# PEER gates: the second index's one-hot made by the scalar engine, and a bank of gates laid out with its tokens side by side

## The chip, the cores and the metric

One Trainium2 chip, one core. The metric is the device time of one execution, in microseconds.

## The reference

A decoder trunk of two layers on 256 tokens with 1024 channels. The change lies in the expert mixer (PEER), which both layers have. Cut to that:

```python
def peer_ffn(hn, wq, subkeys, u_tab, v_tab):
    q = (hn @ wq).reshape(B, T, 8, 2, 64)
    s = jnp.einsum('bthsd,hskd->bthsk', q, subkeys)
    s_top, i_top = lax.top_k(s, 16)
    cand = s_top[..., 0, :, None] + s_top[..., 1, None, :]
    c_top, c_idx = lax.top_k(cand.reshape(B, T, 8, 256), 16)
    i1 = jnp.take_along_axis(i_top[..., 0, :], c_idx // 16, axis=-1)
    i2 = jnp.take_along_axis(i_top[..., 1, :], c_idx % 16, axis=-1)
    expert = i1 * 128 + i2
    gate = jax.nn.softmax(c_top, axis=-1)
    ...
    act = jax.nn.gelu(jnp.einsum('cd,ckd->ck', xc, u_tab[expert]))
    return jnp.einsum('ck,ckd->cd', gate * act, v_tab[expert])
```

Each token has 8 heads x 16 = 128 chosen experts (i1, i2) of 128 x 128, each with a gate.

## The kernel before

The tokens are split. The last 96 are done sparsely: their rows of the tables are gathered by indirect DMA, 128 rows of 4 KB at a time, and DVE multiplies them (class `Sparse`: `fetch` L1310 on POOL, `one` L1337 for u and L1347 for v). The first 160 (`ND`) are done densely: PE multiplies them with all 16384 experts, in 128 blocks of 512 KB of the u table (`u_dense` L248), ScalarE applies gelu (`evac` L1004) into `z` (two tiles `z[0]`, `z[1]` of 64 blocks each, 128 partitions by 64 by 160 tokens), z is multiplied by a mask that holds each token's gates and is zero elsewhere, and PE multiplies z with the 128 blocks of the v table (`v_dense` L1011).

**The mask** is what `gates` makes, 64 blocks (half `hf`) at a time. For a token, entry (i2, i1) of the mask is the sum over its 128 choices of onehot(i2) x gate x onehot(i1): a matmul with the choices on the partitions. `turned` has put the indices and gates with choices on the partitions and tokens in the columns: `i1T`, `i2T`, and the gate as a sum of two fp16 numbers, `gHL`. The work goes in sets of four tokens (`GT`), 40 sets per half. Per set, DVE compares an iota with i2 (L1223, `o2`), with i1 (L1225, `o1`) and multiplies the latter with the two parts of the gate (L1227, `og`). ScalarE converts `o2` to fp8 and turns it so that a token's 128 entries lie together (L1231, `o8`). Four sets later, PE makes a bank of eight tokens (two sets): for each token two matmuls with `o8` as weights and `og` as moving operand, 64 columns out (L1242); at the next set DVE multiplies the bank into z (L1247, the weighing).

**What sets the order.** Within the u and v blocks all engines run in the order in which the code issues. The loop of `peer_and_ple` gives routing and gates a budget per block: a block gives `GATE_NS` = 950, a set uses up 1150, so there is about one set for 1.2 blocks. The gates of the first half are made during u blocks 65 to 127, those of the second half during v blocks 0 to 63:

```python
            if i == HB + 1:
                main.append(self.gates(0, z, l))
            sparse.step(base + i)
            step(self.GATE_NS if i > HB else self.DENSE_NS if sparse.ready else self.ROUTE_NS)
            ps = self.u_dense(base + i, hn)
```

The blocks come through a ring of 10 buffers of 512 KB, filled by SP as PE frees them (`raw_done`, `refill`, `fetch` L166). The gathers have 7 row buffers; `step` spreads them evenly over the blocks and ties the issue of each to the end of a dense block:

```python
        if i in k.last_mm:
            k.tc.add_manual_dep(ins.ins, k.last_mm[i].ins.name, mybir.DependencyInfo(
```

Of the kernel before, what the change touches and what calls it, by code (L numbers as in the profile page):

```python
# [11 lines left out]
F8 = mybir.dt.float8e4  # L12
# [8 lines left out]
T = 256  # L21
# [34 lines left out]
class Trunk:  # L56
# [13 lines left out]
    def setup(self):  # L70
# [34 lines left out]
        self.i2T = per.tile([128, ND], F16, name="i2T")  # L105
# [1067 lines left out]
    def turned(self, rp, fin, gate):  # L1173
# [20 lines left out]
        for i, (t0, n, _) in enumerate(TILES):  # L1194
            s = slice(t0, t0 + n)
            nc.scalar.activation(self.i1T[:, s], b[i][:, 0:n], AF.Copy)
            nc.scalar.activation(self.i2T[:, s], b[i][:, n:2 * n], AF.Copy)

            gs = rp.tile([128, 128], F32, name="rt_gs")[:, :n]
            nc.vector.tensor_scalar(gs, b[i][:, 2 * n:3 * n], GSCALE, None, op0=ALU.mult)  # L1200
            nc.vector.tensor_copy(self.gHL[:, 0, s], gs)
            nc.vector.tensor_tensor(out=self.gHL[:, 1, s], in0=gs, in1=self.gHL[:, 0, s],
                                    op=ALU.subtract)
        yield 1000

    def gates(self, hf, z, l):
# [8 lines left out]
        for i in range(n + lag):  # L1215
            if i < n:
                s = slice(i * GT, i * GT + GT)
                o2, og = [self.strm.tile([128, T], F32, name="sq", bufs=11).bitcast(F16)
                          for _ in range(2)]
                o2 = o2.rearrange("p (e t) -> p e t", t=GT)  # L1220
                og = og.rearrange("p (a e t) -> p a e t", a=2, t=GT)
                o1 = self.strm.tile([128, HB, GT], F16, name="o1", bufs=1)
                tt_(out=o2, in0=self.iota, in1=self.i2T[:, None, s].to_broadcast([128, 128, GT]),  # L1223
                    op=ALU.is_equal)
# [5 lines left out]
                o8 = self.rows.tile([128, GT, 128], F8, name="o8", bufs=6)  # L1230
                nc.scalar.activation(o8.rearrange("p t e -> p e t"), o2, AF.Copy,  # L1231
                                     saturate=False)
                sets[i] = (o8, og)
            k, at = divmod(i - lag, bank)
            if k >= 0 and at == 0:
                ps[k] = self.bank("g", 2)
                for j in range(bank):
                    o8, og = sets.pop(k * bank + j)
                    for t in range(GT):
                        c = (j * GT + t) * HB  # L1240
                        for p in range(2):
                            nc.tensor.matmul(ps[k][:, c:c + HB], o8[:, t], og[:, p, :, t],  # L1242
                                             start=p == 0, stop=p == 1)

            if k >= 0 and at == 1:
                v = z[hf][:, :, k * 8:k * 8 + 8].rearrange("p b t -> p t b")
                nc.vector.scalar_tensor_tensor(v, ps.pop(k).rearrange("p (t b) -> p t b", b=HB),  # L1247
# [201 lines left out]
```

## Time and profile before

| | before |
|---|---|
| median of 3 runs | 1523.9 us (1522.53 to 1526.96) |
| profiled execution | 1528.51 us, its span 1526.7 us |
| PE busy | 1500.7 us, 98% of the span |
| DVE busy | 1140.0 us, 75%, 2749 instructions |
| ACT busy | 684.7 us, 45%, 864 instructions |
| DMA | 514.83 MB, 337 GB/s over the span |
| chain that ended last, by engine | PE 67%, DVE 18%, DMA 13% |
| the gates' matmuls (L1242) | x1280, 5% of the chain |

Times are microseconds unless marked ns. An engine's busy time is a share of a span with several stages, so the stretches have to be read one by one; the chain is followed back from the last instruction to what released each step. PE's matmuls overlap in their pipeline, so their rate is the distance from start to start, not the duration of one.

### The profile page before, as it was taken

To read this page: it belongs to the slowest core of one execution; us is meant where nothing else is said; L and a number is where in the kernel's file an instruction comes from. 1 tells how busy PE (TensorE), PEld (TensorE's weight loads), DVE (VectorE), ACT (ScalarE), POOL (GpSimd) and SP (SyncE) were. 2 spreads that over 40 slices of the span, in tenths; PEclk is the share of its full clock that TensorE was granted. 3 is DMA by queue.
4 is the path that set the end of the run, shared out by engine and by line. 5 is a ranking of instruction groups with operands and counts; after the bars stand their busy time and mean duration, and the time that the engine had idled before them with its cause. 6 is when DMAs were issued, how large, how long until landed. Compare 5 with 4: busy or idle time off the path is not lost.

```text
span 1526.7 us, 30307 instructions
## 1 busy us (share of the span) xinstructions
PE 1500.7 (98%) x11910; PEld 1459.3 (96%) x11910; DVE 1140.0 (75%) x2749; ACT 684.7 (45%) x864; POOL 448.4 (29%) x406
## 2 busy tenths in 40 slices
PE   8999999999999999999999999999999999999997
PEld 8858999999999999999999999999999999999997
DVE  6997699988886888645448699988886788544446
ACT  6478321348873877000027321248872877000025
POOL 0000013343444333444400004343444333443400
PEclk9999999999999999999999999999999999999998
DMA  6603679999999999999994379999999999999980
GB/s 240 231 1 113 232 234 408 408 408 408 408 392 394 404 381 373 408 409 409 409 358 153 117 232 402 408 408 408 409 395 392 408 377 374 407 409 409 408 316 28
DMA packets 141246, 514.83 MB, mean 337 GB/s; under 512 B 15985, under 2 KB 16241, under 8 KB 140593
## 3 DMA queue, kind: packets, MB, share of 16 engines
q1 hardware_dynamic: 84384, 308.42, 52.7%
q0 software_dynamic: 55568, 202.66, 33.8%
q8 instruction: 94, 1.54, 0.4%
q10 hardware_dynamic: 1152, 1.82, 0.4%
q14 instruction: 48, 0.39, 0.1%
HBM read 511.53 MB, written 1.05 MB: 336 GB/s over the span
## 4 chain that ended last, share of the span: by engine, by line
PE 67%; DVE 18%; DMA 13%; issue 1%; ACT 1%; SPq 0%; ACTq 0%; DVEq 0%
PE bank_a L1011 27%; PE bank_a L248 19%; DMA wx<-in_v 10%; PE bank_g L1242 5%; DVE row L1337 4%; PE bank_a L225 3%; PE bank_a L227 3%; PE bank_a L226 3%; DVE rt_tmp L1029 2%; DMA wx<-in_u 1%; PE bank_a L564 1%; DVE rt_ixd L1033 1%; DVE rt_eq L1165 1%; DVE rt_eq L1161 1%; PE bank_a L635 1%
## 5 line engine op out<-in xcount | busy, mean ns | idle before, releaser
L1011 PE MATMUL bank_a<-z,wx 128*128 128x160 f32 x4096 | 576.1, 301 | 2.9
L248 PE MATMUL bank_a<-hn,wx 128*128 128x160 f32 x4096 | 569.4, 300 | 2.4 <-DVE rt_gs L1200 1.2
L1011 PEld LDWEIGHTS bank_a<-z,wx 128*128 128x128 f32 x4096 | 561.0, 191 | 10.0 <-DMA wx<-in_v 9.7
L248 PEld LDWEIGHTS bank_a<-hn,wx 128*128 128x128 f32 x4096 | 558.7, 190 | 4.9 <-DVE rt_gs L1200 1.7
L1231 ACT ACTIVATE o<-sq 128x512 fp8e4<-128x512 f16 x160 | 398.8, 2602 | 46.7 <-DVE sq L1223 46.5
L1310 POOL DMA_INDIRECT row<-in_ur,sp_idx x192 | 228.4, 1190 | 453.0 <-PE bank_a L248 175.9
L1347 DVE SCALAR_TENSOR_TENSOR sp_acc<-row,sp_w,sp_acc 128x1024 f32<-128x1024 f32 x188 | 241.7, 1286 | 152.3 <-DMA row<-in_v,sp_idx 151.6
L1310 POOL DMA_INDIRECT row<-in_v,sp_idx x192 | 212.0, 1104 | 332.6 <-PE bank_a L1011 215.4
L1337 DVE SCALAR_TENSOR_TENSOR row<-row,sp_x 128x1024 f32<-128x1024 f32 x192 | 231.4, 1218 | 32.1 <-DMA row<-in_ur,sp_idx 31.9
L184 ACT ACTIVATE wH<-wx 128x1024 fp32r<-128x1024 f32 (+1 forms) x63 | 65.4, 1042 | 387.8 <-DMA wx<-in_proj 336.4
L1004 ACT ACTIVATE z<-bank_a 128x160 f32<-128x160 f32 x256 | 96.3, 381 | 284.1 <-PE bank_a L248 283.5
L1247 DVE SCALAR_TENSOR_TENSOR z<-bank_g,z 128x512 f32<-128x512 f32 x80 | 93.1, 1164 | 65.5 <-PE bank_g L1242 65.5
L197 DVE TENSOR_TENSOR wL<-wx,wH 128x1024 fp32r<-128x1024 f32 (+1 forms) x63 | 75.9, 1206 | 51.5 <-ACT wH L184 51.0
L225 PE MATMUL bank_a<-hnH,wH 128*128 128x256 f32 x320 | 93.0, 294 | 6.5 <-ACT wH L184 6.0
L227 PE MATMUL bank_a<-hnH,wL 128*128 128x256 f32 x320 | 92.5, 290 | 0.3 <-DVE wL L197 0.3
L226 PE MATMUL bank_a<-hnL,wH 128*128 128x256 f32 x320 | 92.3, 289 | 0.0
L1242 PE MATMUL bank_g<-sq,o 128*128 128x64 f16 x1280 | 89.5, 237 | 0.0
L1242 PEld LDWEIGHTS <-o 128*128 128x128 fp8e4 x1280 | 82.6, 113 | 3.0
L1227 DVE TENSOR_TENSOR sq<-o,gHL 128x512 f16<-128x512 f16 x160 | 68.1, 426 | 11.1
L225 PEld LDWEIGHTS bank_a<-hnH,wH 128*128 128x128 f32 x320 | 62.8, 198 | 7.3 <-ACT wH L184 6.2
L1223 DVE TENSOR_TENSOR sq<-iota,i2T 128x512 f16<-128x512 f16 x160 | 67.3, 421 | 0.0
L227 PEld LDWEIGHTS bank_a<-hnH,wL 128*128 128x128 f32 x320 | 63.0, 197 | 0.7 <-DVE wL L197 0.6
(311 smaller groups left out, 1212.5 us busy)
## 6 DMA issues: line engine op xcount, KB each, us to landing
wx<-in_u SPq DMA_DIRECT2D x256, 512.0 KB, 12.2
wx<-in_v SPq DMA_DIRECT2D x256, 512.0 KB, 11.6
wx<-in_wq SPq DMA_DIRECT2D x16, 512.0 KB, 4.3
wx<-in_gatew SPq DMA_DIRECT2D x16, 512.0 KB, 6.4
wx<-in_win SPq DMA_DIRECT2D x15, 512.0 KB, 4.9
w<-in_cw SPq DMA_DIRECT2D x2, 2048.0 KB
wx<-in_wout SPq DMA_DIRECT2D x8, 512.0 KB, 3.5
row<-in_ur,sp_idx POOLq DMA_INDIRECT x192, 9.6
```

Of the source, the lines that this page charges most:

```text
L225: mm(out, wH, xH, start=start, stop=False, **kw)
L226: mm(out, wH, xL, start=False, stop=False, **kw)
L227: mm(out, wL, xH, start=False, stop=stop, **kw)
L248: m = self.nc.tensor.matmul(out, w[:, kt * 128:kt * 128 + 128], x[:, kt, :ND], start=kt == 0, stop=kt == KT - 1)
L1004: self.nc.scalar.activation(z[i // HB][:, i % HB], ps, AF.Gelu_apprx_tanh)
L1011: m = self.nc.tensor.matmul(acc[kt // 2][:, (kt % 2) * ND:(kt % 2) * ND + ND], w[:, kt * 128:kt * 128 + 128], x, start=b == 0 and kt % 2 == 0,
L1231: nc.scalar.activation(o8.rearrange("p t e -> p e t"), o2, AF.Copy, saturate=False)
L1242: nc.tensor.matmul(ps[k][:, c:c + HB], o8[:, t], og[:, p, :, t], start=p == 0, stop=p == 1)
L1247: nc.vector.scalar_tensor_tensor(v, ps.pop(k).rearrange("p (t b) -> p t b", b=HB), 1.0 / GSCALE, v, op0=ALU.mult, op1=ALU.mult)
L1310: ins = k.nc.gpsimd.indirect_dma_start(out=G, out_offset=None, in_=table, in_offset=bass.IndirectOffsetOnAxis(ap=self.idx[:, c:c + 1], axi ...
L1337: nc.vector.scalar_tensor_tensor(G, G, 1.0, self.x[u], op0=ALU.mult, op1=ALU.mult, accum_out=self.dot[:, col])
L1347: nc.vector.scalar_tensor_tensor(self.acc[u], G, self.w[:, col], self.acc[u], op0=ALU.mult, op1=ALU.add)
```

## The change

The comparison of the second index leaves VectorE. ScalarE makes the one-hot in two steps: for each of the four tokens Abs(iota - i2), with the negated index (`i2n`, now fp32) as bias of each partition, then one Relu(1 - that) over the four. The result is fp16, with a token's 128 entries together, and goes to PE as weights as it is; the conversion to fp8 is gone. The matmul's 64 columns are written eight elements apart in the bank, so that the eight tokens of a block lie side by side, and the weighing reads the bank in order and z in runs of eight.

```diff
-        self.i2T = per.tile([128, ND], F16, name="i2T")
+        self.i2n = per.tile([128, ND], F32, name="i2n")
...
-            nc.scalar.activation(self.i2T[:, s], b[i][:, n:2 * n], AF.Copy)
+            nc.scalar.activation(self.i2n[:, s], b[i][:, n:2 * n], AF.Copy, scale=-1.0)
...
-                o2, og = [self.strm.tile([128, T], F32, name="sq", bufs=11).bitcast(F16)
-                          for _ in range(2)]
-                o2 = o2.rearrange("p (e t) -> p e t", t=GT)
+                og = self.strm.tile([128, T], F32, name="sq", bufs=11).bitcast(F16)
                 og = og.rearrange("p (a e t) -> p a e t", a=2, t=GT)
                 o1 = self.strm.tile([128, HB, GT], F16, name="o1", bufs=1)
-                tt_(out=o2, in0=self.iota, in1=self.i2T[:, None, s].to_broadcast([128, 128, GT]),
-                    op=ALU.is_equal)
...
-                o8 = self.rows.tile([128, GT, 128], F8, name="o8", bufs=6)
-                nc.scalar.activation(o8.rearrange("p t e -> p e t"), o2, AF.Copy,
-                                     saturate=False)
-                sets[i] = (o8, og)
+                ab = self.rows.tile([128, 512], F16, name="ab", bufs=2)
+                for t in range(GT):
+                    nc.scalar.activation(ab[:, t * 128:t * 128 + 128], self.iota[:, :, 0], AF.Abs,
+                                         bias=self.i2n[:, i * GT + t:i * GT + t + 1])
+                o2 = self.strm.tile([128, T], F32, name="sq", bufs=11).bitcast(F16)
+                nc.scalar.activation(o2, ab, AF.Relu, scale=-1.0, bias=self.ones[:, 0:1])
+                sets[i] = (o2.rearrange("p (t e) -> p t e", t=GT), og)
...
-                    o8, og = sets.pop(k * bank + j)
+                    o2, og = sets.pop(k * bank + j)
                     for t in range(GT):
-                        c = (j * GT + t) * HB
+                        o = ps[k].rearrange("p (b t) -> p t b", b=HB)[:, j * GT + t]
                         for p in range(2):
-                            nc.tensor.matmul(ps[k][:, c:c + HB], o8[:, t], og[:, p, :, t],
+                            nc.tensor.matmul(o, o2[:, t], og[:, p, :, t],
                                              start=p == 0, stop=p == 1)
 
             if k >= 0 and at == 1:
-                v = z[hf][:, :, k * 8:k * 8 + 8].rearrange("p b t -> p t b")
-                nc.vector.scalar_tensor_tensor(v, ps.pop(k).rearrange("p (t b) -> p t b", b=HB),
+                v = z[hf][:, :, k * 8:k * 8 + 8]
+                nc.vector.scalar_tensor_tensor(v, ps.pop(k).rearrange("p (b t) -> p b t", b=HB),
                                                1.0 / GSCALE, v, op0=ALU.mult, op1=ALU.mult)
```

ScalarE in the second half of the u blocks, before (L1231 is the conversion, L1004 the evacuation of a dense block; brackets name the engines waited for):

```order
L1004 ACTIVATE z_3607<-bank_a 128x160 [waits PE_49] x2
L1231 ACTIVATE o_3940<-sq 128x128x4 [waits DVE_49,Activation_49]
L1004 ACTIVATE z_3607<-bank_a 128x160 [waits PE_49]
L1231 ACTIVATE o_3979<-sq 128x128x4 [waits DVE_49]
L1004 ACTIVATE z_3607<-bank_a 128x160 [waits PE_49]
```

and now (L1227 the Abs, L1230 the Relu, L1003 the evacuation):

```order
L1227 ACTIVATE ab<-iota,i2n 128x128 x4
L1230 ACTIVATE sq<-ab,ones 128x512 [waits Activation_49]
L1003 ACTIVATE z_3607<-bank_a 128x160 [waits PE_49]
L1227 ACTIVATE ab<-iota,i2n 128x128 x4
L1230 ACTIVATE sq<-ab,ones 128x512 [waits DVE_49,PE_49,Activation_49]
L1003 ACTIVATE z_3607<-bank_a 128x160 [waits PE_49]
```

Where one conversion waited for DVE, four Abs and a Relu stand; they wait for ScalarE itself, and some Relus for a buffer that PE and DVE free.

VectorE at the same place, before (L1223, L1225, L1227 make a set, L1337 takes a gathered row, L1247 is the weighing):

```order
L1223 TENSOR_TENSOR sq<-iota,i2T 128x512
L1225 TENSOR_TENSOR o_3975<-iota,i1T 128x256
L1227 TENSOR_TENSOR sq<-o_3975,gHL 128x512
L1247 SCALAR_TENSOR_TENSOR z_2106<-bank_g,z_2106 128x8x64
L1337 SCALAR_TENSOR_TENSOR row,sp_dot<-row,sp_x_2116 128x1024
L1223 TENSOR_TENSOR sq<-iota,i2T 128x512
L1225 TENSOR_TENSOR o_3999<-iota,i1T 128x256
L1227 TENSOR_TENSOR sq<-o_3999,gHL 128x512
```

and now (L1220, L1222 make a set, L1335 takes a row, L1245 is the weighing):

```order
L1220 TENSOR_TENSOR o_4077<-iota,i1T 128x256
L1222 TENSOR_TENSOR sq<-o_4077,gHL 128x512
L1245 SCALAR_TENSOR_TENSOR z_2106<-bank_g,z_2106 128x64x8
L1335 SCALAR_TENSOR_TENSOR row,sp_dot<-row,sp_x_2116 128x1024
L1220 TENSOR_TENSOR o_4104<-iota,i1T 128x256
L1222 TENSOR_TENSOR sq<-o_4104,gHL 128x512
```

Of a set's three operations the first is gone, and the weighing runs over 64 blocks by 8 tokens instead of 8 tokens by 64 blocks. PE's order is the same row by row, with other operands.

## Rows read from the trace of the kernel before

**Rows 1.** The page: busy us, share of the span, instructions of each engine.

```profile
PE 1500.7 (98%) x11910; PEld 1459.3 (96%) x11910; DVE 1140.0 (75%) x2749; ACT 684.7 (45%) x864; POOL 448.4 (29%) x406
```

**Rows 2.** Stretches: length, busy us of PE, PEld, DVE, ACT, POOL; PEclk, DMA share, GB/s.

```profile
225.00:316.00 91.00, 89.07 (x700) 87.84 (x698) 86.21 (x338) 19.75 (x53) 36.46 (x35) 1.00 1.02 402
330.00:487.00 157.00, 157.00 (x1329) 156.24 (x1329) 126.01 (x256) 109.49 (x104) 66.57 (x53) 1.00 1.02 401
487.00:616.00 129.00, 129.00 (x1123) 128.24 (x1122) 105.84 (x176) 100.20 (x46) 45.33 (x43) 1.00 1.01 388
```

**Rows 3.** The chain of waits within the v half: start us, us, what.

```profile
534.43 0.96 PE bank_g L1242 x16
535.39 4.40 PE bank_a L1011 x32
```

**Rows 4.** Groups by line: operation, out<-in, count | busy us, mean ns | idle before.

```profile
L1242 PE MATMUL bank_g<-sq,o 128*128 128x64 f16 x1280 | 89.5, 237 | 0.0
L1242 PEld LDWEIGHTS <-o 128*128 128x128 fp8e4 x1280 | 82.6, 113 | 3.0
L1231 ACT ACTIVATE o<-sq 128x512 fp8e4<-128x512 f16 x160 | 398.8, 2602 | 46.7 <-DVE sq L1223 46.5
L1223 DVE TENSOR_TENSOR sq<-iota,i2T 128x512 f16<-128x512 f16 x160 | 67.3, 421 | 0.0
L1247 DVE SCALAR_TENSOR_TENSOR z<-bank_g,z 128x512 f32<-128x512 f32 x80 | 93.1, 1164 | 65.5 <-PE bank_g L1242 65.5
L1004 ACT ACTIVATE z<-bank_a 128x160 f32<-128x160 f32 x256 | 96.3, 381 | 284.1 <-PE bank_a L248 283.5
```

**Rows 5.** POOL in order of time, v half: start us, us, instruction [idle before <-releaser].

```profile
569.01 1.02 POOL L1310 DMA_INDIRECT row<-in_v,sp_idx  x1 [2.25 <-DVE sp_acc L1347]
571.19 0.94 POOL L1310 DMA_INDIRECT row<-in_v,sp_idx  x1 [1.16 <-DVE sp_acc L1347]
574.37 0.94 POOL L1310 DMA_INDIRECT row<-in_v,sp_idx  x1 [2.25 <-PE bank_a L1011]
578.72 0.94 POOL L1310 DMA_INDIRECT row<-in_v,sp_idx  x1 [3.41 <-PE bank_a L1011]
```

**Rows 6.** Stretches of 20 us late in the v blocks, columns as in rows 2.

```profile
680.00:700.00 20.00, 20.00 (x150) 20.00 (x149) 9.81 (x8) 0.00 (x0) 8.63 (x9) 1.00 1.03 408
720.00:740.00 20.00, 19.42 (x133) 18.03 (x133) 9.46 (x9) 0.00 (x0) 9.37 (x7) 1.00 1.03 409
740.00:760.00 20.00, 19.54 (x137) 18.43 (x136) 8.70 (x8) 0.00 (x0) 8.24 (x8) 1.00 1.03 409
760.00:780.00 20.00, 19.65 (x141) 18.93 (x140) 5.07 (x4) 0.00 (x0) 0.58 (x1) 1.00 1.02 410
```

**Rows 7.** Groups by line and shape on ACT and DVE, columns as in rows 4.

```profile
L436 ACT ACTIVATE dg<-ident,cvec 128x128 f32<-128x128 f32 x14 | 5.3, 395 | 4.0 <-PE bank_g L437 4.0
L264 ACT ACTIVATE hnH<-h,vecs 128x256 fp32r<-128x256 f32 x32 | 14.9, 499 | 15.2 <-DVE h L945 13.0 <-DMA vecs<-in_vecs 1.3 <-DMA h<-in_xT 0.6
L282 ACT ACTIVATE sqs<-h 128x256 f32<-128x256 f32 x38 | 14.8, 405 | 2.8 <-DVE h L968 2.8
L1153 ACT ACTIVATE rt_key<-rt_ixd 128x512 f16<-128x512 uint32 x4 | 2.5, 615 | 0.0
L388 DVE TENSOR_TENSOR o<-bank_r,o 128x512 f32<-128x512 f32 x4 | 2.5, 685 | 1.2 <-PE bank_r L329 1.2
```

**Rows 8.** PE in order of time, the queries' projection: start us, us, instruction.

```profile
169.73 0.28 PE L225 MATMUL bank_a<-hgH,wH 128*128 128x256 f32 x1
169.85 0.28 PE L226 MATMUL bank_a<-hgL,wH 128*128 128x256 f32 x1
```

**Rows 9.** Weight loads by line and shape, columns as in rows 4.

```profile
L637 PEld LDWEIGHTS <-identb 128*128 128x128 bf16 x12 | 1.2, 98 | 2.9 <-issue 2.9
```

**Rows 10.** The chain of waits at the end of layer 0's v blocks.

```profile
786.11 3.49 PE bank_r L1358 x32
```

**Rows 11.** Waits from 487 to 616 us: us in total, times, longest us.

```profile
DVE z L1247 <- PE bank_g L1242: 15.8, 12, 3.0
```

More of the change, by code (lines that the diff above doesn't have):

```diff
@@ L11 @@
 F16 = mybir.dt.float16
-F8 = mybir.dt.float8e4
 BF16 = mybir.dt.bfloat16
```

## The prediction, made before any run of the changed kernel

> **What bounds the kernel now.** Read first the busy times of the engines over the whole span [rows 1]: TensorE 1500.7 us of 1526.7, VectorE 1140.0, ScalarE 684.7. A share over the whole span hides the stages, so next come the stretches in which the gates are made and applied [rows 2]: the second half of the u blocks of layer 0 (330 to 487 us) and the first half of its v blocks (487 to 616 us). In both, PE is busy for every microsecond (157.00 of 157, 129.00 of 129), while DVE has 105.84 and ACT 100.20 of the 129. The transfers stand at 401 and 388 GB/s, under the 408 that they reach elsewhere [rows 6]. So these stretches are set by PE. The row of 225 to 316 us is different: there DVE has 86.21 of 91, with the routing, but the gates are first made in the second half of the u blocks, so the change cannot touch it.
>
> The chain of waits [rows 3] shows what PE does in such a stretch: 32 dense matmuls in 4.40 us (137 ns each, 2.2 us for a block of 16), then one bank of gates, 16 matmuls in 0.96 us, and so on with no gap. That is **60 ns for one gate pair** (load of weights and matmul), and 1280 pairs make 77 us of the span. Only this number can move the time directly. The gate operations on the other engines [rows 4] are large in sum but lie beside PE: DVE even waits for PE before the weighing, 15.8 us in the v half of layer 0 [rows 11].
>
> After 616 us the gates are over; PE runs at full rate on the blocks fetched ahead (150 matmuls in 20 us) until these are used up, and then waits for transfers: 133, 137 and 141 matmuls in three stretches of 20 us, at 409 GB/s [rows 6]. Short by 17 + 13 + 9 = 39 matmuls of 0.136 us, this is 5.3 us a layer, some 10.6 us in both.
>
> **VectorE.** The comparison for the second index goes: 160 x 0.421 = 67.3 us [rows 4]. The weighing of 128x512 now reads the bank in order and z in runs of eight. It takes 1164 ns [rows 4]; the nearest row with a bank and an SBUF operand side by side in that size is 685 ns [rows 7]. I take that: 80 x 0.479 = 38 us; at the other end it stays at 1164, because z still jumps after every eighth element, and gives nothing. DVE should come to about 1034 us. None of it is on the path: in the gate stretches DVE has 23 us to spare of 129 and waits for PE. Cost on the path: 0.
>
> **ScalarE.** Out goes the conversion, 160 x 2602 ns (398.8 us busy, so 2.49 each with the overlap of neighbours) [rows 4]. In come, per set of four tokens, four Abs of 128x128 with a bias per partition and one Relu of 128x512. A 128x128 activation from SBUF with an operand per partition takes 395 ns [rows 7]; less 0.11 of overlap, four are 1.14 us. A 128x512 to f16 takes 615 ns, and the operand per partition adds 499 - 405 = 94 [rows 7]: 0.71 us. Sum 1.85 us for 2.49, ACT from 685 to about 582 us. Without any overlap it is 4 x 0.395 + 0.71 = 2.29 us, still under 2.49. The set no longer waits for DVE, but the Relu waits for its own four Abs and, every second time, for the PE bank before it; the next evacuation of a dense block stands behind it, with four banks to spare. Cost on the path: 0, as long as a set takes less than the 129 / 40 = 3.2 us that PE leaves it in the v half.
>
> **TensorE.** The order of its instructions stays as it was; two things differ within a gate pair. First the weights: 128x128 of fp16 instead of fp8. Loading fp8 takes 113 ns on average [rows 4], and loading 128x128 of bf16, also two bytes, 98 ns [rows 9]; I take no change. Upper bound: fp32 weights, four bytes, under small matmuls, 3.49 us for 32 pairs, 109 ns each [rows 10], which is 49 ns more for three bytes more, so 16 ns for one byte and 1280 x 16 = 21 us. Lower bound: 15 ns less, as 98 is less than 113, minus 19 us. [...]
>
> Second the output: the 64 columns of a matmul now land eight elements apart in the bank. No PE output in this trace is spread like that, so bounds. A 256-column matmul of split halves starts every 120 ns [rows 8], 0.47 ns a column; 64 columns are 30 ns, half of the 60 of a gate pair. A dense fp32 matmul does 160 columns in 137 ns [rows 3], 0.86 ns each; 64 at that slow rate are 55 ns, again inside 60. So columns may leave at half the fast rate at no cost; at a quarter of it a pair is 120 ns, plus 60 x 1280 = 77 us. I take no change, since both rates that the trace shows fit under the pair; ends 0 and +77 us.
>
> **The gathers.** A faster DVE frees row buffers sooner, so do gathers run ahead? The issues of POOL [rows 5] come at 569.01, 571.19, 574.37 and 578.72 us, that is 2.18, 3.18 and 4.35 us apart: one block, one block and a bank, two blocks. They beat time with PE's blocks, to which the code ties them, also where the profile names DVE as the last to release. So nothing for the transfers.
>
> **Sum**: 0 (VectorE) + 0 (ScalarE) + 0 (TensorE) + 0 (gathers). The profiled execution took 1528.51 us (its span of 1526.7 and 1.8 around it), 4.6 us above the median of the three runs; on that execution 1528.5 stays 1528.5, and as a median **1523.9 us**.
>
> **Rivals.** *Spread output slows the gate matmul (slower).* Place: the 80 banks. It decides as soon as a column takes more than 0.94 ns, since 64 of them then pass 60 ns; at a quarter of the fast rate +77 us, 1601 us; at 1.2 ns a column, 77 ns a pair, +22 us, 1546 us. For it: PE has no slack there, each ns goes 1280 times into the time. Against: a factor of two is already covered. [...] Chance 0.16.
>
> *Weights of two bytes load longer (slower)*: +21 us, 1545 us; decides where the load, not the matmul, sets the 60 ns. Against it the 98 ns. Chance 0.05.
>
> *ScalarE becomes the bound (slower).* The Abs reads every fourth element of the iota. The conversion, which writes with a jump, takes 2602 where a plain 128x512 takes 615 [rows 4, 7], 3.9 ns more per element; were the jumping read as dear, an Abs is 0.89 and a set 4.27 us, over the 3.2 us: 40 x 4.27 = 171 us for the 129 of the v half, and with 64 evacuations of 381 ns [rows 4] 195 for the 157 of the u half, 80 us a layer, 1684 us. Against: a step of 8 bytes is far less than the 128 of that write. Chance 0.04.
>
> *Transfers gain (faster).* If gathers after all come earlier, PE's shortfall after 700 us goes: at most 10.6 us, 1513 us. Against: [rows 5]. Chance 0.06.
>
> *A gate pair gets shorter (faster)*: by up to 15 ns with the two-byte load, 19 us, 1505 us. Chance 0.04.
>
> That the weighing stays at 1164 ns, so that the second half of the change does not do what it says, would leave the time alone, and is part of the first case.
>
> **Numbers.** A measurement of this kernel tells 0.3%, 4.6 us, from no change. No change 0.65; slower 0.16 + 0.05 + 0.04 = 0.25; faster 0.06 + 0.04 = 0.10. The range reaches down to 1512, over the whole transfer case, and up to 1548, over the weight case and the cheaper part of the spread output (pairs up to 79 ns, some 0.06): 0.65 + 0.06 + 0.05 + 0.06 = 0.82.
>
> **What would show it.** Right: in the chain a gate bank of 16 still takes 0.95 us and 32 dense matmuls 4.40; DVE near 1034 us with 160 instructions fewer and the weighing near 685 ns; ACT near 582 us with 640 instructions more, an Abs near 395 ns and a Relu near 709; the gate stretches end at 616 us as now. Wrong: a bank that takes over 1 us (spread output, or weights, then with a longer load), an Abs over 0.6 us with PE waiting for ACT, or more than 133 matmuls in the 20 us after 720 us.

## The result and the profile after

The changed kernel takes **1518.07 us** (median of 11 runs, 1515.91 to 1521.57) against 1526.41 us for the kernel before in as many runs beside it (1522.53 to 1530.56). The ratio is 0.9947, with a 95% interval of 0.9934 to 0.9959: **faster by 0.5%, some 8 us**. The forecast was no change; the time lies in the range of 1512 to 1548 us, but on a side that had 0.10.

The engines' work came out nearly as predicted. The page of the profile after, busy time and instructions of each engine, and the shares of the chain that ended last [rows 1]:

```profile
PE 1494.1 (99%) x11910; PEld 1457.3 (96%) x11910; DVE 1051.0 (69%) x2589; ACT 609.5 (40%) x1504; POOL 432.9 (29%) x406
...
PE 74%; DVE 18%; DMA 6%; issue 1%; ACT 1%; SPq 0%; DVEq 0%; ACTq 0%
```

DVE has 160 instructions fewer and ACT 640 more. The chain's share of DMA is 6%, where it was 13%. The groups of the gates' lines (operation, count, then busy us, mean ns, idle before), to be read against [rows 4]:

```profile
L1227 ACT ACTIVATE ab<-iota,i2n 128x128 f16<-128x128 f16 x640 | 208.4, 398 | 0.0
L1003 ACT ACTIVATE z<-bank_a 128x160 f32<-128x160 f32 x256 | 76.3, 302 | 320.0 <-PE bank_a L247 311.7
L1245 DVE SCALAR_TENSOR_TENSOR z<-bank_g,z 128x512 f32<-128x512 f32 x80 | 55.2, 691 | 151.6 <-PE bank_g L1240 146.0
L1230 ACT ACTIVATE sq<-ab,ones 128x512 f16<-128x512 f16 x160 | 115.5, 722 | 84.0 <-issue 66.9
...
L1240 PE MATMUL bank_g<-sq 128*128 128x64 f16 x1280 | 89.7, 240 | 0.0
L1240 PEld LDWEIGHTS <-sq 128*128 128x128 f16 x1280 | 82.8, 114 | 3.0
```

The Abs takes 398 ns (predicted 395), the Relu 722 (709), the weighing 691 (685). The gate matmul and its load of weights are as they were, 240 and 114 ns for 237 and 113. Next the gate stretches and those after them (length, busy us of PE, PEld, DVE, ACT, POOL; PEclk, DMA share, GB/s), against [rows 2, 6]:

```profile
225.00:314.00 89.00, 87.43 (x689) 86.37 (x687) 85.47 (x332) 19.81 (x53) 37.08 (x35) 1.00 1.02 412
328.00:484.00 156.00, 156.00 (x1321) 155.24 (x1321) 102.42 (x211) 91.24 (x257) 57.26 (x53) 1.00 1.01 400
484.00:613.00 129.00, 129.00 (x1123) 128.24 (x1122) 85.33 (x139) 80.00 (x206) 47.33 (x43) 1.00 1.00 388
...
680.00:700.00 20.00, 20.00 (x150) 20.00 (x149) 9.76 (x8) 0.00 (x0) 9.17 (x8) 1.00 1.03 418
720.00:740.00 20.00, 19.84 (x142) 19.12 (x141) 9.74 (x8) 0.00 (x0) 7.49 (x8) 1.00 1.03 418
740.00:760.00 20.00, 19.86 (x141) 18.94 (x140) 9.46 (x8) 0.00 (x0) 7.90 (x6) 1.00 1.03 417
760.00:780.00 20.00, 20.00 (x150) 20.00 (x149) 2.64 (x3) 0.78 (x1) 0.58 (x1) 1.00 0.97 389
```

In the two stretches with gates PE is busy throughout, as before. DVE fell from 105.84 to 85.33 us in the second, ACT from 100.20 to 80.00, and it bought nothing there. The difference stands in the rows below, where **there is no gate work at all**: 417 to 418 GB/s for 408 to 409, and 142 and 141 matmuls for 133 and 137 in the stretches from 720 to 760 us. Even 225 to 314 us, before any gate is made, has 412 for 402.

The chain of waits says how much time this is. Of the changed kernel (start us, us, what), around the first gate bank, the last bank of layer 0's v half, the matmuls L1356 that close the sparse part, and the same two in layer 1:

```profile
336.00 0.96 PE bank_g L1240 x16
...
607.93 4.40 PE bank_a L1010 x32
612.33 0.96 PE bank_g L1240 x16
613.29 8.75 PE bank_a L1010 x64
...
780.65 3.49 PE bank_r L1356 x32
...
1298.80 11.33 PE bank_a L1010 x83
...
1466.27 3.49 PE bank_r L1356 x32
```

A bank of 16 still takes 0.96 us and 32 dense matmuls 4.40. From the first bank to the end of the last one it is 613.29 - 336.00 = 277.29 us; from the rows of the kernel before, below, 615.88 - 338.68 = 277.20. From the end of the gates to the closing matmuls it is 780.65 - 613.29 = 167.36 us in layer 0 and 1466.27 - 1298.80 = 167.47 in layer 1. The same places in the kernel before (L1358 closes there, in layer 0 from 786.11 us on [rows 10]):

```profile
338.68 0.95 PE bank_g L1242 x16
...
615.88 6.17 PE bank_a L1011 x45
...
1305.26 4.81 PE bank_a L1011 x35
...
1476.28 3.49 PE bank_r L1358 x32
```

That is 170.23 and 171.02 us: 2.87 + 3.55 = 6.42 us of the 10.4 between the two spans (1526.7 and 1516.3). Another 2.68 us had come by the first gate bank. Of these 1.47 lie before the first matmul of the u blocks (at 181.28 and 179.81 us), a part that takes 179.1 to 184.1 us in the traces of this document, wherever the buffers lie, and so does not count for the change; the other 1.21 lie between that matmul and the first gate bank, and 0.94 more at the same place in layer 1. So the gain lies where transfers limit PE, and the transfers got faster by 2% (417 to 418 GB/s for 408 to 409, in the rows from 680 to 760 us).

The transfers' own work is the same: the profile's page has 514.83 MB before and 514.86 after. Nor do gathers come earlier against PE. Their issues on POOL (start us, us, instruction, idle before) keep the beat of [rows 5], 3.18, 2.18 and 3.18 us apart, a block and a bank, a block, a block and a bank:

```profile
563.22 0.94 POOL L1308 DMA_INDIRECT row<-in_v,sp_idx  x1 [1.21 <-PE bank_a L1010]
566.40 0.96 POOL L1308 DMA_INDIRECT row<-in_v,sp_idx  x1 [2.25 <-PE bank_a L1010]
568.58 1.31 POOL L1308 DMA_INDIRECT row<-in_v,sp_idx  x1 [1.21 <-PE bank_a L1010]
571.76 0.94 POOL L1308 DMA_INDIRECT row<-in_v,sp_idx  x1 [1.88 <-DVE o L1220]
```

### The profile page after: what moved, and what is told of

Read it like the earlier page. It is cut to its first block, busy times and chain, and to the rows that moved or that the text cites. A ratio compares the mean times of both kernels' runs of the same rounds, so it can differ in the third digit from the quotient of the medians.

```text
span 1516.3 us, 30760 instructions
## 1 busy us (share of the span) xinstructions
PE 1494.1 (99%) x11910; PEld 1457.3 (96%) x11910; DVE 1051.0 (69%) x2589; ACT 609.5 (40%) x1504; POOL 432.9 (29%) x406
## 2 busy tenths in 40 slices
DMA packets 141249, 514.86 MB, mean 340 GB/s; under 512 B 15984, under 2 KB 16240, under 8 KB 140592
## 4 chain that ended last, share of the span: by engine, by line
PE 74%; DVE 18%; DMA 6%; issue 1%; ACT 1%; SPq 0%; DVEq 0%; ACTq 0%
PE bank_a L1010 32%; PE bank_a L247 20%; PE bank_g L1240 5%; DMA wx<-in_v 5%; DVE row L1335 4%; PE bank_a L224 3%; PE bank_a L225 3%; PE bank_a L226 3%; DVE rt_tmp L1028 2%; PE bank_a L563 1%; DVE rt_ixd L1032 1%; DVE rt_eq L1164 1%; DVE rt_eq L1160 1%; PE bank_a L634 1%; DVE rt_eq L1157 1%
## 5 line engine op out<-in xcount | busy, mean ns | idle before, releaser
L1308 POOL DMA_INDIRECT row<-in_ur,sp_idx x192 | 210.8, 1098 | 468.2 <-PE bank_a L247 271.0
L1335 DVE SCALAR_TENSOR_TENSOR row<-row,sp_x 128x1024 f32<-128x1024 f32 x192 | 231.3, 1219 | 35.8 <-DMA row<-in_ur,sp_idx 34.6
L1227 ACT ACTIVATE ab<-iota,i2n 128x128 f16<-128x128 f16 x640 | 208.4, 398 | 0.0
L1003 ACT ACTIVATE z<-bank_a 128x160 f32<-128x160 f32 x256 | 76.3, 302 | 320.0 <-PE bank_a L247 311.7
L1245 DVE SCALAR_TENSOR_TENSOR z<-bank_g,z 128x512 f32<-128x512 f32 x80 | 55.2, 691 | 151.6 <-PE bank_g L1240 146.0
L1230 ACT ACTIVATE sq<-ab,ones 128x512 f16<-128x512 f16 x160 | 115.5, 722 | 84.0 <-issue 66.9
L1240 PE MATMUL bank_g<-sq 128*128 128x64 f16 x1280 | 89.7, 240 | 0.0
L1240 PEld LDWEIGHTS <-sq 128*128 128x128 f16 x1280 | 82.8, 114 | 3.0
L1222 DVE TENSOR_TENSOR sq<-o,gHL 128x512 f16<-128x512 f16 x160 | 68.0, 425 | 9.6
```

Of the source, the lines that this page charges most:

```text
L1003: self.nc.scalar.activation(z[i // HB][:, i % HB], ps, AF.Gelu_apprx_tanh)
L1227: nc.scalar.activation(ab[:, t * 128:t * 128 + 128], self.iota[:, :, 0], AF.Abs, bias=self.i2n[:, i * GT + t:i * GT + t + 1])
L1230: nc.scalar.activation(o2, ab, AF.Relu, scale=-1.0, bias=self.ones[:, 0:1])
L1240: nc.tensor.matmul(o, o2[:, t], og[:, p, :, t], start=p == 0, stop=p == 1)
L1308: ins = k.nc.gpsimd.indirect_dma_start(out=G, out_offset=None, in_=table, in_offset=bass.IndirectOffsetOnAxis(ap=self.idx[:, c:c + 1], axi ...
L1335: nc.vector.scalar_tensor_tensor(G, G, 1.0, self.x[u], op0=ALU.mult, op1=ALU.mult, accum_out=self.dot[:, col])
```

## The experiments

**Where the buffers lie.** One thing in the diff has nothing to do with work: `i2T` (160 two-byte elements, 320 bytes of a partition) became `i2n` (160 four-byte elements, 640 bytes). All that is placed behind it moves up by 320 bytes. The buffers into which the rows are gathered, seven of 4096 bytes, begin at byte 41664 of a partition in the built kernel before, and at 41984 in the changed one; the first is 192 more than a multiple of 256, the second is a multiple of 256 (82 x 512). The ring of ten dense blocks, placed from the other end, begins at 188384 in both, 224 more than a multiple of 256. Buffers of one kind are 4096 bytes apart, so all share that remainder. Below, a destination that begins on a multiple of 256 is called clean, and one that does not is called off.

**Theory A** is that this placement sets the rate of the transfers. **Theory B** is that DVE and ACT, with less to do, leave the transfers more room; **theory C** that the two profiles differ by chance. Pads (tiles that nobody uses) tell them apart: they move buffers and change no work. Each run is compared with the kernel before in runs of the same session; the verdict rests on the ratio and on the stretch from 680 to 700 us, columns as above, in which the kernel before has 408 GB/s [rows 6]. Line numbers shift by one or two with a pad.

### First set: placement or work

`e1`, the kernel before with the rows where the change puts them:

```diff
         self.gHL = per.tile([128, 2, ND], F16, name="gHL")
+        per.tile([128, 160], F16, name="pad")
```

> The kernel before with 320 unused bytes behind gHL, so that the buffers of the gathered rows (and of the dense ring's first three blocks) lie at byte 41984 of a partition, a multiple of 512, as they do in the changed kernel, and not at 41664 (192 more than a multiple of 512). Nothing of the change's work is in it. Theory A, placement: the transfers run at 416 to 418 GB/s in the stretches 680:700 to 740:760 and the time is the changed kernel's, 1516 to 1520 us. Theory B, the transfers gained because VectorE and ScalarE do less during the gates: 408 to 410 GB/s and 1526 us, as before. Theory C, the two profiles differ by chance of the chip: also 1526 us, and a rate that need not be either.

Measured: 1520.95 us, 1 us above the range expected; ratio 0.9944 (0.9923 to 0.9966).

```profile
680.00:700.00 20.00, 20.00 (x149) 20.00 (x148) 9.75 (x8) 0.00 (x0) 9.49 (x9) 1.00 1.03 418
```

The whole gain by the ratio, without any of the change's work, at the changed kernel's rate.

`e2`, the changed kernel with the rows off again:

```diff
         self.gHL = per.tile([128, 2, ND], F16, name="gHL")
+        per.tile([128, 96], F16, name="pad")
```

> The changed kernel with 192 unused bytes behind gHL: the buffers of the rows lie at byte 42176, again 192 more than a multiple of 512. All of the change's work is in it. Theory A: the gain is gone, 1524 to 1528 us, with 408 to 410 GB/s in the stretches 680:700 to 740:760. Theory B: 1516 to 1520 us and 416 to 418 GB/s, as in the changed kernel. Theory C: a gain of any size that does not follow the placement.

Measured: 1528.51 us, ratio 1.0006 (0.9991 to 1.0020).

```profile
680.00:700.00 20.00, 20.00 (x149) 20.00 (x149) 9.48 (x8) 0.00 (x0) 10.94 (x9) 1.00 1.03 409
```

The gain is gone with all of the work in place: theories B and C fall. This kernel and the changed one differ by 192 unused bytes and nothing else, so its chain of waits, at the places shown above, measures the placement alone:

```profile
337.33 0.96 PE bank_g L1241 x16
...
614.74 7.39 PE bank_a L1011 x54
...
785.24 3.49 PE bank_r L1357 x32
...
1303.93 6.17 PE bank_a L1011 x45
...
1474.46 3.49 PE bank_r L1357 x32
```

From the gates' end to the closing matmuls 170.50 and 170.53 us, for 167.36 and 167.47: **3.14 + 3.06 us**. The first bank comes 1.33 us later. Together that is 7.53 of the 8.3 us between the spans of the two (1524.6 and 1516.3).

`e3` and `e4`, the second destination: the dense ring on a multiple of 512, in the changed kernel (so both are) and in the kernel before (so the ring alone is). The same edit in both:

```diff
+        self.ctx.enter_context(self.pool("padr", side="right")).tile([128, 240], F16, name="padr")
         self.ring = self.ctx.enter_context(self.pool("ring", side="right")), RINGS[1], set()
```

> The changed kernel with 480 unused bytes above the second ring of dense weights, so that its ten blocks begin at byte 187904, a multiple of 512, and not at 188384 (480 more than one); the rows stay at 41984. Theory A: if placement also counts for blocks that are read in one piece, a further gain, at most as much for each byte as the rows gave; the dense blocks are most of the bytes, so 1490 to 1515 us, and above 420 GB/s in 680:700. If placement counts for the gathered rows alone: 1518 us and 416 to 418 GB/s. Theory B: 1518 us.

> The kernel before with the ring of dense weights at byte 187904, the rows at 41664 as before. Theory A with both kinds of transfer: between 1495 and 1523 us, the same step as between the changed kernel and the changed kernel with its ring moved. Theory A with the rows alone: 1526 us and 408 to 410 GB/s. Theory B: 1526 us.

Measured: `e3` 1518.99 us, ratio 0.9944 (0.9925 to 0.9963); `e4` 1517.33 us, ratio 0.9926 (0.9904 to 0.9948).

```profile
680.00:700.00 20.00, 20.00 (x150) 20.00 (x148) 9.26 (x8) 0.00 (x0) 9.51 (x8) 1.00 1.03 418
```

```profile
680.00:700.00 20.00, 20.00 (x150) 20.00 (x149) 9.56 (x8) 0.00 (x0) 9.42 (x9) 1.00 1.02 418
```

A surprise for theory A as it stood: moving the ring alone gives all of the gain, and moving both gives no more than one, where 1490 to 1515 us was expected. In `e3` five of six 20-us stretches between 640 and 760 us show 419 GB/s, which is 1 or 2 over the changed kernel, and no time comes of it.

### Second set: which remainders

Rows and ring together were slow at remainders 192 and 480 of 512 and fast at (0, 480), (0, 0) and (192, 0). Either one clean start is enough (A1), or the distance of the two counts (A2). `f1` and `f2` set these against each other with other pads above the ring (144 elements in the kernel before, 96 in the changed one), `f3` and `f4` try other rows (32 and 128 elements behind gHL in the changed kernel):

```diff
+        self.ctx.enter_context(self.pool("padr", side="right")).tile([128, 144], F16, name="padr")
```

```diff
+        self.ctx.enter_context(self.pool("padr", side="right")).tile([128, 96], F16, name="padr")
```

```diff
+        per.tile([128, 32], F16, name="pad")
```

```diff
+        per.tile([128, 128], F16, name="pad")
```

> The kernel before with 288 unused bytes above the second dense ring: rows at 41664 (192 more than a multiple of 512, as before), ring at 188096 (also 192 more). So far the rate was 408 to 410 GB/s with rows 192 and ring 480 over a multiple of 512, and 416 to 419 with rows 0 and ring 480, rows 0 and ring 0, rows 192 and ring 0. Theory A1, one of the two destinations must begin on a multiple of 512 and here neither does: 408 to 410 GB/s in 680:700 and 1524 to 1529 us. Theory A2, the distance between the two destinations counts, modulo 512 (224 was slow; 32, 0 and 192 were fast), and here it is 0: 416 to 419 GB/s and 1516 to 1520 us.

> The changed kernel with 192 unused bytes above the second dense ring: rows at 41984 (a multiple of 512), ring at 188192 (288 more than one). Theory A1, one aligned destination is enough: 416 to 418 GB/s and 1516 to 1520 us. Theory A2: the distance is 224 modulo 512, that of the kernel before, so 408 to 410 GB/s and 1524 to 1529 us.

> The changed kernel with 64 unused bytes behind gHL: rows at 42048 (64 more than a multiple of 512), ring at 188384 (480 more, unmoved). Theory A1 with 512 as the size that counts: neither is aligned, 408 to 410 GB/s and 1524 to 1529 us. With 64 as the size that counts, 416 to 418 GB/s (but then the kernel before, at 192, should have been fast too). Theory A2: distance 96, which lies between two fast ones, so 416 to 418 GB/s and 1516 to 1520 us.

> The changed kernel with 256 unused bytes behind gHL: rows at 42240 (256 more than a multiple of 512), ring at 188384 (unmoved). Theory A1 with 512 as the size that counts: 408 to 410 GB/s and 1524 to 1529 us; with 256 or 128: 416 to 418 GB/s and 1516 to 1520 us. Theory A2: distance 288, not yet seen, either.

Measured: `f1` 1526.96 us, ratio 0.9989 (0.9975 to 1.0003); `f2` 1517.22 us, 0.9920 (0.9900 to 0.9941); `f3` 1528.25 us, 0.9999 (0.9982 to 1.0015); `f4` 1517.64 us, 0.9920 (0.9901 to 0.9940).

```profile
680.00:700.00 20.00, 20.00 (x149) 20.00 (x148) 9.33 (x8) 0.00 (x0) 10.32 (x9) 1.00 1.03 409
```

```profile
680.00:700.00 20.00, 20.00 (x149) 20.00 (x149) 9.75 (x8) 0.00 (x0) 10.31 (x9) 1.00 1.03 418
```

```profile
680.00:700.00 20.00, 20.00 (x149) 20.00 (x148) 9.12 (x9) 0.00 (x0) 10.42 (x9) 1.00 1.03 409
```

```profile
680.00:700.00 20.00, 20.00 (x149) 20.00 (x148) 9.74 (x8) 0.00 (x0) 9.79 (x9) 1.00 1.02 417
```

The distance is nothing: `f1` has distance 0 and is slow (409 GB/s), `f2` has that of the kernel before and is fast (418). Rows at remainder 64 are slow (409) and at 256 fast (417), so 512 is not the size that counts; 128 or 256 is.

### Third set: the size, and the parts of the change by themselves

`g1` puts the rows at remainder 128 (changed kernel, 64 elements behind gHL), `g2` the ring at remainder 256 with the rows off (kernel before, 112 elements above the ring):

```diff
+        per.tile([128, 64], F16, name="pad")
```

```diff
+        self.ctx.enter_context(self.pool("padr", side="right")).tile([128, 112], F16, name="padr")
```

> The changed kernel with 128 unused bytes behind gHL: rows at 42112 (128 more than a multiple of 512), ring at 188384 (480 more). Rows at 0 and 256 over a multiple of 512 were fast with this ring, rows at 64 and 192 slow. If rows have to begin on a multiple of 128: 416 to 418 GB/s in 680:700 and 1516 to 1520 us. If on a multiple of 256: 408 to 410 GB/s and 1524 to 1529 us.

> The kernel before with 224 unused bytes above the second dense ring: rows at 41664 (192 more than a multiple of 512, slow), ring at 188160 (256 more). If an aligned ring is enough whatever the rows are, and 128 or 256 is the size that counts for it as for the rows: 416 to 419 GB/s and 1516 to 1520 us. If only a multiple of 512 counts for the ring: 408 to 410 GB/s and 1524 to 1529 us.

Measured: `g1` 1527.74 us, ratio 1.0006 (0.9992 to 1.0020); `g2` 1518.11 us, 0.9945 (0.9928 to 0.9962).

```profile
680.00:700.00 20.00, 20.00 (x149) 20.00 (x149) 9.65 (x8) 0.00 (x0) 8.97 (x9) 1.00 1.03 409
```

```profile
680.00:700.00 20.00, 20.00 (x150) 20.00 (x149) 9.35 (x9) 0.00 (x0) 8.56 (x8) 1.00 1.03 418
```

So **a multiple of 256 bytes** it is, for the rows as tried at 64, 128 and 192 (409 GB/s) and at 256 (417); for the ring 0 and 256 are fast (418 GB/s) and 192 and 480 slow (408 to 409), with the rows off. The ring was not tried at 128 with the rows off, so for the ring alone a multiple of 128 is not excluded.

`g3` is the kernel before with the bank's new layout alone, no buffer moved; `g4` the scalar engine's one-hot alone, with the bank as before and the rows off by 192:

```diff
-                        c = (j * GT + t) * HB
+                        o = ps[k].rearrange("p (b t) -> p t b", b=HB)[:, j * GT + t]
...
-                            nc.tensor.matmul(ps[k][:, c:c + HB], o8[:, t], og[:, p, :, t],
+                            nc.tensor.matmul(o, o8[:, t], og[:, p, :, t],
...
-                v = z[hf][:, :, k * 8:k * 8 + 8].rearrange("p b t -> p t b")
-                nc.vector.scalar_tensor_tensor(v, ps.pop(k).rearrange("p (t b) -> p t b", b=HB),
+                v = z[hf][:, :, k * 8:k * 8 + 8]
+                nc.vector.scalar_tensor_tensor(v, ps.pop(k).rearrange("p (b t) -> p b t", b=HB),
```

In `g4` these same lines are turned back in the changed kernel, and behind gHL stands

```diff
+        per.tile([128, 96], F16, name="pad")
```

> The kernel before with the second part of the change alone: the gate matmul writes a bank with its tokens side by side and the weighing runs over neighbouring elements; the one-hot of the second index is made as before and every buffer lies where it lay. The prediction's sum: the weighing falls from 1164 to about 690 ns, off the path; the gate bank stays at 0.96 us; 408 to 410 GB/s; 1524 to 1529 us. If the change's gain came from VectorE's work after all: half of it or so, 1520 to 1524 us. If spread columns cost the gate matmul something that the one-hot's part gave back: a bank above 1.0 us and over 1529 us.

> The first part of the change alone, with 192 unused bytes behind gHL so that rows and ring are again 192 and 480 over a multiple of 512: the one-hot of the second index made by Abs and Relu on ScalarE, the gate matmul's columns contiguous and the weighing strided as in the kernel before. The prediction's sum: 1524 to 1529 us, 408 to 410 GB/s, VectorE some 67 us less than before, the gate bank at 0.96 us. If the gain came from the engines' work: 1518 to 1523 us.

Measured: `g3` 1526.53 us, ratio 1.0002 (0.9989 to 1.0016); `g4` 1527.98 us, 1.0002 (0.9984 to 1.0020). The stretch, then the weighing's group and (`g3`) the chain at the last bank of the v half of layer 0. First `g3`:

```profile
680.00:700.00 20.00, 20.00 (x149) 20.00 (x149) 9.07 (x9) 0.00 (x0) 9.76 (x9) 1.00 1.03 409
```

```profile
L1247 DVE SCALAR_TENSOR_TENSOR z<-bank_g,z 128x512 f32<-128x512 f32 x80 | 55.2, 690 | 100.3 <-PE bank_g L1242 100.0
```

```profile
609.37 4.40 PE bank_a L1011 x32
613.77 0.96 PE bank_g L1242 x16
```

And `g4`, with its evacuation of a dense block too:

```profile
680.00:700.00 20.00, 20.00 (x150) 20.00 (x149) 9.74 (x8) 0.00 (x0) 9.20 (x9) 1.00 1.03 409
```

```profile
L1004 ACT ACTIVATE z<-bank_a 128x160 f32<-128x160 f32 x256 | 76.6, 303 | 324.5 <-PE bank_a L248 324.0
L1246 DVE SCALAR_TENSOR_TENSOR z<-bank_g,z 128x512 f32<-128x512 f32 x80 | 92.7, 1159 | 120.0 <-PE bank_g L1241 120.0
```

Both parts do what they say (690 ns for the weighing in `g3`; 160 comparisons gone from DVE in `g4`, 1088.3 us busy for 1140.0) and **neither is worth anything by itself**. A bank with spread columns takes 0.96 us with fp8 weights as well, so no cost of the spread is hidden by a gain of the weights; in `g4`, with fp16 weights and columns side by side, the chain has 0.96 us too.

### Fourth set: the destinations or what lies beside them

The pads above had moved more than the buffer that they name: the one behind gHL also the first half of z, the one above the ring also the second half of z, the sums and the index lists, each by the same bytes. With the cause that far open, the next four move one without the other, all in the kernel before. `h1`, the rows, with the scratch tiles that lie between gHL and them (what follows them goes on by 512 bytes in all):

```diff
+        per.tile([128, 160], F16, name="pad")
...
             self.rows = self.ctx.enter_context(self.pool("rows"))
+            self.ctx.enter_context(self.pool("padz")).tile([128, 96], F16, name="padz")
```

`h2`, z and the rest, but not the rows:

```diff
             self.rows = self.ctx.enter_context(self.pool("rows"))
+            self.ctx.enter_context(self.pool("padz")).tile([128, 160], F16, name="padz")
```

`h3`, the ring alone, and `h4`, what lies below it but not the ring (there with 240 elements in `padb` and no `padr`):

```diff
+        self.ctx.enter_context(self.pool("padr", side="right")).tile([128, 240], F16, name="padr")
         self.ring = self.ctx.enter_context(self.pool("ring", side="right")), RINGS[1], set()
+        self.ctx.enter_context(self.pool("padb", side="right")).tile([128, 16], F16, name="padb")
```

> The kernel before with the rows moved to 41984 by 320 unused bytes behind gHL, and 192 more behind the rows, so that the first half of z and all that follows it lie 512 bytes further, that is as before modulo 512. If the destination of the gathered rows counts: 416 to 418 GB/s in 680:700 and 1516 to 1520 us. If the place of z and the scratch behind the rows counts: 408 to 410 GB/s and 1524 to 1529 us.

> The kernel before with the rows unmoved at 41664 and 320 unused bytes behind them, so that the first half of z begins at 73728, a multiple of 512, as it does in the changed kernel. If the destination of the rows counts: 408 to 410 GB/s and 1524 to 1529 us. If z counts: 416 to 418 GB/s and 1516 to 1520 us.

> The kernel before with the dense ring moved to 187904, a multiple of 512, by 480 unused bytes above it, and 32 more below it, so that the second half of z, the sums and the index lists lie 512 bytes lower, that is as before modulo 512. If the destination of the dense blocks counts: 416 to 419 GB/s and 1516 to 1520 us. If what lies below the ring counts: 408 to 410 GB/s and 1524 to 1529 us.

> The kernel before with the dense ring unmoved at 188384 and 480 unused bytes below it, so that the second half of z, the sums and the index lists move as they did with the ring. If the destination of the dense blocks counts: 408 to 410 GB/s and 1524 to 1529 us. If what lies below the ring counts: 416 to 419 GB/s and 1516 to 1520 us.

Measured: `h1` 1517.68 us, ratio 0.9936 (0.9912 to 0.9961); `h2` 1526.18 us, 0.9992 (0.9978 to 1.0006); `h3` 1518.64 us, 0.9942 (0.9922 to 0.9962); `h4` 1526.78 us, 0.9996 (0.9982 to 1.0011).

```profile
680.00:700.00 20.00, 20.00 (x149) 20.00 (x149) 9.38 (x9) 0.00 (x0) 10.13 (x9) 1.00 1.03 418
```

```profile
680.00:700.00 20.00, 20.00 (x149) 20.00 (x148) 9.75 (x8) 0.00 (x0) 8.90 (x8) 1.00 1.03 409
```

```profile
680.00:700.00 20.00, 20.00 (x149) 20.00 (x149) 9.26 (x9) 0.00 (x0) 10.45 (x9) 1.00 1.03 418
```

```profile
680.00:700.00 20.00, 20.00 (x150) 20.00 (x149) 9.15 (x8) 0.00 (x0) 9.78 (x8) 1.00 1.03 409
```

It is the **destinations of the transfers** and not z, the sums or the index lists beside them. The scratch between gHL and the rows moved in `h1` too; in `j1` and `j2` below it stays, and the rate follows the rows.

### Fifth set: whole kinds or a share of the packets

Why is one clean kind of transfer enough? In `j1` and `j2` (the changed kernel) the ring stays off and the row buffers stand 4224 or 4160 bytes apart, so that four or two of the seven begin on a multiple of 256:

```diff
-        G = k.rows.tile([128, D], F32, name="row", bufs=ROWBUFS)
+        G = k.rows.tile([128, D + 32], F32, name="row", bufs=ROWBUFS)[:, :D]
```

```diff
+        G = k.rows.tile([128, D + 16], F32, name="row", bufs=ROWBUFS)[:, :D]
```

> The changed kernel with row buffers 4224 bytes apart and not 4096: from 41984 on, the first, third, fifth and seventh begin on a multiple of 256, the others 128 beside one; the ring unmoved. So 4/7 of the rows' half of the bytes, some 28% of all, begin on a multiple of 256; with the rows wholly so it was about half, and 417 to 418 GB/s, with none 408 to 409. If the share counts in proportion up to that half: 413 to 414 GB/s in 640:660 and 680:700, and 1520 to 1524 us. If a kind of transfer has to be clean as a whole: 408 to 410 GB/s and 1524 to 1529 us. If far less than half is enough: 416 to 418 GB/s and 1516 to 1520 us.

> The changed kernel with row buffers 4160 bytes apart: from 41984 on, the first and the fifth begin on a multiple of 256, the others 64, 128 or 192 beside one; the ring unmoved. So some 14% of all bytes begin on a multiple of 256. In proportion: 411 to 412 GB/s and 1522 to 1527 us. As a whole kind: 408 to 410 GB/s and 1524 to 1529 us. If little is enough: 416 to 418 GB/s and 1516 to 1520 us.

Measured: `j1` 1522.37 us, ratio 0.9976 (0.9966 to 0.9985); `j2` 1523.15 us, 0.9980 (0.9971 to 0.9990).

```profile
680.00:700.00 20.00, 20.00 (x150) 20.00 (x149) 9.76 (x8) 0.00 (x0) 9.39 (x9) 1.00 1.03 414
```

```profile
680.00:700.00 20.00, 20.00 (x150) 20.00 (x149) 9.74 (x8) 0.00 (x0) 8.90 (x8) 1.00 1.03 412
```

So the share counts, and in proportion, as far as three steps show it: with 0, some 14, some 28 and about half of the bytes on a multiple of 256 the rate is 408 to 409, 412, 414 and 417 to 418 GB/s, about 2 for every 10%. The second half adds 1 at most. The times follow: 3 to 4 us of the 8, though the two are too near each other to be told apart by time. The distance between the buffers changed along with the share; a run with the buffers further apart and all of them clean is missing.

All placements, remainders by 256 (the dense ring's and the rows' first buffer):

| kernels | rows | ring | GB/s, 680 to 700 us | ratio to before |
|---|---|---|---|---|
| before, `e2`, `g3`, `g4`, `h2`, `h4` | 192 | 224 | 408 to 409 | 0.9992 to 1.0006 |
| `f1` | 192 | 192 | 409 | 0.9989 |
| `f3` | 64 | 224 | 409 | 0.9999 |
| `g1` | 128 | 224 | 409 | 1.0006 |
| `j2` | 2 of 7 at 0 | 224 | 412 | 0.9980 |
| `j1` | 4 of 7 at 0 | 224 | 414 | 0.9976 |
| after, `e1`, `f4`, `h1` | 0 | 224 | 417 to 418 | 0.9920 to 0.9947 |
| `f2` | 0 | 32 | 418 | 0.9920 |
| `e4`, `g2`, `h3` | 192 | 0 | 418 | 0.9926 to 0.9945 |
| `e3` | 0 | 0 | 418 | 0.9944 |

No kernel of these beats the changed one by more than the intervals leave open. The traces agree on the place of the gain: from the end of the gates to the closing matmuls it is 170 to 173 us, in either layer, in the nine kernels with both destinations off, and 167 to 169 us in the nine with one or both clean.

## Why the prediction was wrong

**The step that failed** is the account of what the change moves. "The gathers ... So nothing for the transfers" asked when the transfers are issued, and not where they land; the sum had no term for the 320 bytes by which the wider `i2n` shifts the row buffers. That term is worth the whole result, 0.6% or 8 to 9 us by the ratios: in the changed kernel, where it goes with the placement (`e2`), and in the kernel before, where it comes with it (`e1`). The same step is behind the sentence that the change cannot touch 225 to 316 us [rows 2]: that row rose from 402 to 412 GB/s.

**The gathers' timing** was right as far as it went: the issues kept PE's beat [rows 5]. The rival "transfers gain" had the right place (PE's shortfall after 700 us, 5.3 us a layer, [rows 6]) and a bound of 10.6 us that holds, but named earlier issues as the mechanism and got 0.06. With 418 GB/s PE is short of 8 + 9 + 0 matmuls in the three late stretches and not of 39: 22 x 0.136 = 3.0 us a layer, near the 2.87 to 3.55 read from the chains.

**VectorE**, off the path: right. 160 x 0.421 and 80 x 0.473 us, 105 in all, went from its groups, as forecast. Its busy time fell by 89.0 us, to 1051 and not to 1034: the sum took the comparison at its full 421 ns, but it overlaps with its neighbour (in the kernel before one runs from 344.75 us for 0.42, and the next comparison starts at 345.09), and where it alone goes (`g4`) the busy time falls by 51.7 us and not by 67.3. `g3` and `g4` show a worth of nothing on the path, within 0.2%.

**ScalarE**, off the path: right. 609.5 us for the predicted 582: the Abs were taken at 0.285 us each with their overlap, 182 us for 640, and the group has 208.4. All of it was covered, with 80.00 of 129 us busy in the v half.

**TensorE**, gate pair unchanged at 60 ns: right. Spread columns and two-byte weights together leave a bank at 0.96 us and the load at 114 ns, so the slower rivals (0.16 and 0.05) did not come; nor did the shorter pair (0.04). Nor does either cost anything alone: a bank takes 0.96 us with the spread columns and fp8 weights (`g3`), and 0.96 with fp16 weights and the columns side by side (`g4`).

**The range** held because it reached over the whole transfer case. That is luck: the mechanism for which it was drawn so wide did not come. Nor is the miss the 5.8 us between 1523.9 and 1518.07: the forecast was of no change, its 1523.9 was the median of only three runs, and the change is 8.3 us. **What would show it** worked: more than 133 matmuls in the 20 us after 720 us (142) was written down as the sign of a wrong forecast.

**The size that counts**, 256 bytes, comes from the runs, as does that it is the destination's (`h1` to `h4`): with the ring off, rows at remainders 64, 128 and 192 gave one rate, 409 GB/s (`f3`, `g1`, `e2`), and rows at 0 gave 417 to 418 (the changed kernel, `f4`). How far beside the multiple a start lies made no difference among these three. With both kinds clean the rate is 419 GB/s (`e3`) over 409, 2.4% more. A cost for each packet by itself would give half of the gain for one clean kind, where one gave nearly all, 417 to 418. The averages of the packets in each queue show the same. From 640 to 720 us (a queue's share of 16 engines x 80 us, over its packets) a packet takes 146 ns on average in either queue of the kernel before (52.3% for 4589 of the dense blocks, 50.0% for 4370 of the gathers). It takes 143 in either queue both of the changed kernel, where only the rows are clean (52.9% for 4734, 49.3% for 4425), and of `e4`, where only the ring is (53.2% for 4776, 49.1% for 4390). By these averages, packets that still land off are shortened as much as the clean ones.

**Left open**: how a clean packet helps one that is off, and why the gain levels off once about half of the bytes are clean. The highest rate read over 20 us is 419 GB/s (`e3`, `e4`, `h3`); whether the transfers have a second limit there, no run tests. Nor was it tried whether the transfers' sources in HBM play a part.

## What to carry to other kernels

Let the buffers that large transfers write (here 4096 bytes to a partition) begin on a multiple of 256 bytes of a partition, first of all where a stage runs at the transfers' ceiling (here 408 to 409 GB/s with both kinds off, 417 to 419 with one or both clean); a pad of a few hundred bytes was enough, and here it was worth 0.6% with no other edit (`e1`, ratio 0.9944). When a change adds or widens a tile, list which buffers behind it move, and count that as a part of the change. And before a gain is put down to the work that was saved, run the old kernel with the new placement, and the new one with the old.

## What was not expected of the hardware

- The destination's start sets the transfers' ceiling in the mix of gathers and dense blocks: 408 to 409 GB/s with both off a multiple of 256, 417 to 419 with one or both on it, and between them in proportion to the share (412 and 414 with some 14% and 28% of the bytes on it, `j2` and `j1`).
- The evacuation of a dense block by ACT became shorter though nothing in it changed: 302 ns for 381 [rows 4], and 303 in `g4`, but 371 in `g3`, which keeps the conversion to fp8. So the longer evacuation goes with the conversion on the same engine. It costs ACT no time that shows: in the kernel before, an evacuation right behind a conversion starts while that still runs (start us, us, instruction):

```profile
344.67 2.52 ACT L1231 ACTIVATE o<-sq 128x512 fp8e4<-128x512 f16 x1
346.67 0.65 ACT L1004 ACTIVATE z<-bank_a 128x160 f32<-128x160 f32 x1
```

The second starts 0.52 us before the first ends and outlasts it by 0.13. Nor are the 20 us by which its group fell (96.3 to 76.3) to be found in ACT's busy time: without the conversion and with Abs and Relu it would be 684.7 - 398.8 + 208.4 + 115.5 = 609.8 us, and it is 609.5. What the evacuation does while the conversion runs, no run shows.

- A gate matmul that writes 64 columns eight elements apart costs the same as one that writes them side by side (0.96 us a bank of 16 in `g3`, for 0.95 to 0.96 in the kernel before).
- Transfers share the cost: a packet that lands off a multiple of 256 takes 143 ns on average for 146, from 640 to 720 us, when the other kind's packets are clean (the dense blocks' in the changed kernel, the gathers' in `e4`).
